# Two moves in the order of a two-layer trunk kernel: the gates at the end of the seventh scan step, the second out-projection round behind the second head's queries and keys

## The chip, the cores and the metric

The kernel runs on one core of a Trainium2 chip. A core has TensorE (PE: matrix products from SBUF into PSUM, with the weight loads shown as PEld), VectorE (DVE), ScalarE (ACT), GpSimd (POOL), and DMA queues; SyncE (SP) and ACT issue the transfers here. Every engine works off its own list of instructions in a fixed order, and semaphores hold an instruction until what it needs is there. The metric is the device time of one execution in microseconds (us); lower is better.

## The reference

A decoder trunk of two residual layers over x with 512 tokens of 1024 channels, in float32. The first layer is a mixer with two halves that read one projection of the normed input: a state-space scan (SSD: 16 heads in 2 groups, with a causal convolution, a decay, a gate z and a norm per group) and a gated linear attention (GLA: 4 heads, with queries, keys, values, a forget gate in the logarithm and an output gate). Both halves go through one output projection. The second layer is latent attention with 16 heads. A dense SwiGLU block follows each. What matters here, cut from the reference:

```python
def ssd_gla_layer(h, w_in, ...):
    z, xbc, dt_raw, q, k, v, g, gk_low = jnp.split(h @ w_in, ...)
    y_ssd = ssd_mixer(z, xbc, dt_raw, ...)        # conv, scan, * silu(z), rms_norm per group of 512
    y_gla = gla_mixer(q, k, v, g, gk_low, ...)
    return jnp.concatenate([y_ssd, y_gla], axis=-1) @ w_out

def gla_mixer(q, k, v, g, gk_low, gk_w2, gk_b, norm_w):
    gk = jax.nn.log_sigmoid(gk_low @ gk_w2 + gk_b) / 16
    gcum = jnp.cumsum(gk over chunks of 64)
    q_dec, k_inv = q * exp(gcum), k * exp(-gcum); k_end = k * exp(g_last - gcum)
    ...  # scores inside a chunk, states across chunks
    return rms_norm(o, norm_w) * silu(g)
```

## The kernel before

Activations lie with channels on the 128 partitions and the 512 tokens along the free axis, so x is eight tiles X[0..7] of 128 x 512. Every dense product is made from three products of a high and a low float32r part (mm3, lines 159 to 162: L160, L161, L162 in the profile), which keeps float32 accuracy. A weight piece is loaded by SP (L148, a buffer of two, wraw), its high part is cast by ACT (L154, whi), its low part subtracted by DVE (L155, wlo; both with three buffers). A product of 128 output channels goes over eight such triples (24 products) into one PSUM bank of the pool acc, which has three banks (NACC); an out-projection piece of 256 columns covers two banks of twelve products each.

The mixer runs in this order of the code:

- Eight scan steps f = 0 to 7 (lines 554 to 579; the eighth is called step 7 and the seventh step 6 here). Each has a conv (L387 to L402: product, L392 scales it into xpad, three taps L397, tanh, and xs at L402), a z gate (L424 to L428 and gate(), L276: zh reads the product), and the core (L430 to L492: decays mt from ACT at L444 and L446, the products L456, L467, L481, L485, and the result y at L491). After step 3 and after step 7 a group norm (L494 to L500 with rstd, L184 to L208) scales the four y of the group and splits them into parts mxh and mxl (L136, L137): the inputs of one out-projection round.
- In step 7, behind the z gate: gates() (L524 to L551) computes the logarithmic forget gates of all GLA heads. It loads a small weight with three DMAs on ACT's queue, splits it, makes four products (L539) into one auxiliary bank, takes Abs (L540), Exp (L543) and Ln (L545) on ACT, the minimum (L541), the difference (L547) and eight running sums (L551) on DVE, and leaves the result in gm. Then comes round 0 of the out-projection (out_round, L296 to L306), which adds 8 banks of products to X (L304), and the values of GLA head 2.
- The GLA heads: inner(h) (L590 to L688) makes queries, keys, scores, states, and the normed output of head h; outer(h) (L690 to L699) multiplies it by the output gate and splits it. Round 1 of the out-projection is called from inside inner(0), behind its queries and keys (after_dense, L636).

The order on each engine is not written out. A scheduler plays the program once when the kernel is built and gives each engine the ready instruction that stands first in the code; weights are ranked 90 instructions (AHEAD) earlier than they stand. Buffers of one tag are handed out in the order of the code. Three things follow that matter around the change. First, gates() borrows buffers of the scan: gw and wt carry the tag cvt of the conv's tanh, w2 the tag cva, and the two ga tiles the tag mt of the decays, each tag with two buffers. Second, the tiles of the heads (pool gla) lie where those of the scan (pool ssd) lay, so the first of them can only be written when the scan's tiles are done with, the group norm's last among them. Third, a round of the out-projection needs PSUM banks of acc, like every dense product.

Of the kernel before, what the change touches and what calls it, by code (L numbers as in the profile page):

```python
# [30 lines left out]
NACC = 3  # L31
PROJ = (0, 2)
R0F = 7


PV = {}
# [12 lines left out]
def kernel(ctx: ExitStack, tc: tile.TileContext, A, yT, stop=99):  # L49
# [11 lines left out]
    def nm(s):  # L61
        cnt[0] += 1
        return f"{s}_{cnt[0]}"

    def acc():
        return pacc.tile([P, T], F32, tag="acc", name=nm("acc"))
# [11 lines left out]
    def aux(tag="st"):  # L78
        while isinstance(phase["tags"][tag], str):
            tag = phase["tags"][tag]  # L80
        return phase["p"].tile([P, T], F32, tag=tag, name=nm(tag), bufs=phase["tags"][tag])
# [23 lines left out]
    def col(name, i=0, lo=0, hi=P):  # L105
        j = PV[name] + i
        return pv[lo:hi, j:j + 1]
# [32 lines left out]
    def weight(src, kc, m):  # L140

        with tc.high_priority(offset=AHEAD):
            return weight_now(src, kc, m)
# [20 lines left out]
    def dense(ps, w, xs):  # L164

        n = len(xs)
        for k, (xh, xl) in enumerate(xs):
            last = mm3(ps, w[0][:, k, :], w[1][:, k, :], xh, xl, k == 0, k == n - 1)
        return last
# [94 lines left out]
    def tok_scalar(R):  # L264

        ps = aux()
        for c in range(4):
            E.transpose(ps[:, c * P:(c + 1) * P], R[:, c * P:(c + 1) * P], ident)
        r = const.tile([P, 4], F32, tag="rtok", name=nm("rtok"))
        V.tensor_copy(r, ps.rearrange("p (c x) -> p c x", c=4)[:, :, 0])  # L270
        return r
# [24 lines left out]
    def out_round(r, parts, nxt=None):  # L296

        for m2 in range(4):
            w = weight(A["w_out"][r, m2], 4, 256)
            for j in range(2):  # L300
                m = 2 * m2 + j
                ps = acc()
                dense(ps, (w[0][:, :, j * P:(j + 1) * P], w[1][:, :, j * P:(j + 1) * P]), parts)
                V.tensor_tensor(X[m], X[m], ps, ALU.add)  # L304
                if nxt is not None:
                    nxt.add(m)  # L306
# [8 lines left out]
    with tc.tile_pool(name="gkp", bufs=1) as gkp:  # L315
# [62 lines left out]
        with tc.tile_pool(name="ssd", bufs=2) as sp:  # L378
# [6 lines left out]
            def conv(i, tag, bufs, bank=acc):  # L385

                w = weight(A["w_xbc"][i], KD, P)  # L387
                ps = bank()
                mm[i] = dense(ps, w, xp)
                xpad = sp.tile([P, T + 3], F32, tag="xpad", name=nm("xpad"))  # L390
                G.memset(xpad[:, 0:3], 0.0)
                V.tensor_tensor(xpad[:, 3:], ps, R, ALU.mult)  # L392
                a = sp.tile([P, T], F32, tag="cva", name=nm("cva"))
                S.activation(a, xpad[:, 3:], AF.Identity, bias=cw[:, 48 + i:49 + i],
                             scale=cw[:, 36 + i:37 + i])
                for k in range(3):
                    V.scalar_tensor_tensor(a, xpad[:, k:k + T], cw[:, 12 * k + i:12 * k + i + 1], a,  # L397
                                           ALU.mult, ALU.add)
                t = sp.tile([P, T], F32, tag="cvt", name=nm("cvt"))
                S.activation(t, a, AF.Tanh)  # L400
                o = sp.tile([P, T], F32, tag=tag, name=nm(tag), bufs=bufs)
                V.scalar_tensor_tensor(o, t, 1.0, a, ALU.add, ALU.mult)  # L402
                return o

            def group(g):

                bank = (lambda: aux("a2")) if g == 0 else acc
                bT = conv(8 + g, "bT", 1, bank)
                cT = conv(10 + g, "cT", 2, bank)
                ps = aux("a1")  # L410
                for c in range(4):
                    E.matmul(ps[:, c * P:(c + 1) * P], bT[:, c * P:(c + 1) * P],
                             cT[:, c * P:(c + 1) * P], start=True, stop=True)
                cb = sp.tile([P, 4, P], F32, tag="cb", name=nm("cb"), bufs=1)
                V.tensor_tensor(cb, ps.rearrange("p (c l) -> p c l", c=4),
                                tri.unsqueeze(1).to_broadcast([P, 4, P]), ALU.mult)
                ps = aux("a1")
                for c in range(3):
                    E.transpose(ps[:, c * P:(c + 1) * P], bT[:, c * P:(c + 1) * P], ident)
                btok = sp.tile([P, 3, P], F32, tag="btok", name=nm("btok"), bufs=1)  # L420
                S.copy(btok, ps[:, :3 * P].rearrange("p (c l) -> p c l", c=3))
                return cb, cT, btok

            def z_gate(f):  # L424
                w = weight(A["w_z"][f], KD, P)
                ps = acc()
                dense(ps, w, xp)
                return gate(sp, "z", ps, R, 2)  # L428
# [65 lines left out]
            def group_norm(g, ys, ssq):  # L494
                Rg = rstd(ssq, 512, sp, "Rg")
                parts = []
                for j, y in enumerate(ys):
                    V.scalar_tensor_tensor(y, y, col("ssd_norm", 4 * g + j), Rg, ALU.mult, ALU.mult)
                    parts.append(to_parts(y))
                return parts  # L500
# [23 lines left out]
            def gates():  # L524

                gw = sp.tile([80, T], F32R, tag="cvt", name="gw")
                G.memset(gw.bitcast(I32), 0)
                w2 = sp.tile([P, T], F32, tag="cva", name="w2")
                wt = sp.tile([P, T], F32R, tag="cvt", name="wt")
                for j in (0, 32, 64):  # L530
                    nc.scalar.dma_start(w2[j:j + 16, :], A["gk_w2"])
                S.copy(wt[0:16, :], w2[0:16, :])
                V.tensor_tensor(gw[0:16, :], w2[0:16, :], wt[0:16, :].bitcast(F32), ALU.subtract)
                for j in (32, 64):
                    S.copy(gw[j:j + 16, :], w2[j:j + 16, :])
                gas = [sp.tile([P, 2, T], F32, tag="mt", name=nm("ga")) for _ in range(2)]
                for h in range(4):
                    ps = aux()
                    E.matmul(ps, gw[:, h * P:(h + 1) * P], gx, start=True, stop=True)  # L539
                    S.activation(gas[h // 2][:, h % 2, :], ps, AF.Abs, bias=col("gk_b", h))  # L540
                    V.tensor_scalar(gm[:, h, :], ps, col("gk_b", h), 0.0, ALU.add, ALU.min)  # L541
                for ga in gas:
                    S.activation(ga, ga, AF.Exp, scale=-1.0)  # L543
                for ga in gas:
                    S.activation(ga, ga, AF.Ln, bias=1.0)  # L545
                for j, ga in enumerate(gas):
                    V.tensor_tensor(gm[:, 2 * j:2 * j + 2], gm[:, 2 * j:2 * j + 2], ga, ALU.subtract)  # L547
                for h in range(4):
                    for t0 in (0, T // 2):
                        gj = gm[:, h, t0:t0 + T // 2]  # L550
                        V.tensor_tensor_scan(gj, rmask, gj, 0.0, ALU.mult, ALU.add)  # L551

            rounds = []
            for f in range(8):
                g = f // 4
                if f % 4 == 0:
                    bc = group(g)
                    ys, ssq = [], None
                xs = conv(f, "xs", 3)
                if f == 0:  # L560
                    with tc.high_priority(offset=STEPS):
                        dt, act, acd = steps(mm[0])
                zg = z_gate(f)
                if f == R0F:
                    gates()
                    out_round(0, rounds[0])
                if f == VALUES[0]:
                    rtok = tok_scalar(R)
                if f in VALUES:
                    values(VALUES.index(f))  # L570
                y = core(f, xs, zg, *bc)
                ys.append(y)
                sq = res.tile([P, T], F32, tag="sq", name=nm("ysq"), bufs=2)
                S.activation(sq, y, AF.Square)
                if ssq is not None:
                    V.tensor_tensor(sq, ssq, sq, ALU.add)
                ssq = sq
                if f % 4 == 3:
                    rounds.append(group_norm(g, ys, ssq))


        with tc.tile_pool(name="gla", bufs=2) as gp:
# [115 lines left out]
                    parts.append(to_parts(os[e]))  # L698
                return parts  # L699

            o0 = inner(0, lambda: out_round(1, rounds[1]))
            o1 = inner(1)
            p01 = outer(0, o0)
            o2 = inner(2)
            p01 += outer(1, o1)
# [56 lines left out]
    with tc.tile_pool(name="mla", bufs=2) as mp, tc.tile_pool(name="mla1", bufs=1) as m1:  # L762
# [41 lines left out]
        for who, n0, n in (("q", 0, 3), ("kv", 3, 2)):  # L804
# [23 lines left out]
            f = rsqrt(m1, lm, [P, 4], "lr", who)  # L828
# [278 lines left out]
```

## Time and profile before

| what | value |
|---|---|
| median of 3 runs | 1379.67 us (1378.09 to 1379.68) |
| the profiled execution: its own time | 1377.99 us |
| its span in the trace | 1375.8 us |
| mean granted clock of TensorE | 0.996 |
| PE busy | 1347.7 us (98%) |
| DVE busy | 814.3 us (59%) |
| ACT busy | 571.5 us (42%) |
| scan steps, gates, round 0 and head queries in the trace | up to about 228 us |
| round 1 in the trace | from 236 us |

How to read it: a row of a timeline is start, duration, engine, line, operation, output and inputs by the program's names, shapes, how many instructions were merged, and in brackets the idle time of the engine before it with what ended it. A start-to-start distance of products is their cost, as their durations overlap. In a waits row, the columns are total us, times, and the longest. Busy shares are means over the whole program, which has stages with very different limits; what a change in one stage is worth is read from that stage.

### The profile page before, as it was taken

How to read it: one execution, taken by the hardware profiler on the slowest of the kernel's cores; microseconds unless marked ns; L12 is line 12 of the kernel's file. 1: busy time of each engine (PE TensorE's matmuls, PEld its weight loads, DVE VectorE, ACT ScalarE, POOL GpSimd, SP SyncE). 2: the span in 40 equal slices, each digit the busy share in tenths (PEclk: the TensorE clock that was granted, in tenths of full speed). 3: DMA queues.
4: the chain of work that ended last, by engine and by line, in shares of the span. 5: the costliest groups of instructions: out<-in, count | busy, mean ns of one | idle time of the engine just before them, and what ended most of it. 6: DMA issues, size and time to landing. Idle time of an engine off the chain costs nothing.

```text
span 1375.8 us, 16690 instructions
## 1 busy us (share of the span) xinstructions
PE 1347.7 (98%) x6506; PEld 1089.3 (79%) x6506; DVE 814.3 (59%) x1369; ACT 571.5 (42%) x950; POOL 7.8 (1%) x35
## 2 busy tenths in 40 slices
PE   9999997999999999999999999999999999999998
PEld 5798886888788888888888887667588888888887
DVE  7877987597768444444333469776594444443221
ACT  7665563344334323223223248774652332332221
POOL 0000000000000000000000000000000000000000
PEclk9999998999999999999999999999999999999999
DMA  5342232222232233233333311111023323333331
GB/s 175 126 138 78 77 98 75 61 62 82 78 102 92 92 100 100 92 104 97 90 90 104 101 60 65 47 47 62 1 92 99 101 92 96 104 92 107 108 105 64
DMA packets 36782, 122.23 MB, mean 89 GB/s; under 512 B 4768, under 2 KB 5792, under 8 KB 36704
## 3 DMA queue, kind: packets, MB, share of 16 engines
q1 hardware_dynamic: 35888, 120.72, 28.1%
q8 instruction: 51, 0.84, 0.3%
q10 hardware_dynamic: 816, 0.46, 0.1%
q14 instruction: 27, 0.22, 0.1%
HBM read 119.03 MB, written 2.13 MB: 88 GB/s over the span
## 4 chain that ended last, share of the span: by engine, by line
PE 91%; DVE 5%; ACT 2%; issue 1%; DMA 0%; SPq 0%; DVEq 0%; ACTq 0%
PE acc L161 27%; PE acc L160 27%; PE acc L162 27%; PE sco L960 2%; PE ptr L974 1%; PE po L983 1%; DVE wlo L155 1%; PE a L481 1%; PE a L673 1%; PE a L467 0%; PE a L662 0%; PE a L485 0%; DMA x<-in_xT_dram 0%; ACT whi L154 0%; PE a L675 0%
## 5 line engine op out<-in xcount | busy, mean ns | idle before, releaser
L154 ACT CAST whi<-wraw 128x1024 fp32r<-128x1024 f32 (+2 forms) x221 | 225.8, 1022 | 556.8 <-PE acc L161 422.8
L160 PE MATMUL acc<-xh,whi 128*128 128x512 f32 x1144 | 448.7, 393 | 2.8 <-ACT qT L943 1.6
L161 PE MATMUL acc<-xl,whi 128*128 128x512 f32 x1144 | 448.6, 392 | 0.0
L162 PE MATMUL acc<-xh,wlo 128*128 128x512 f32 x1144 | 448.0, 392 | 0.0
L155 DVE TENSOR_TENSOR wlo<-wraw,whi 128x1024 fp32r<-128x1024 f32 (+2 forms) x221 | 262.0, 1186 | 155.3 <-ACT whi L154 155.1
L160 PEld LDWEIGHTS acc<-xh,whi 128*128 128x128 f32 x1144 | 214.7, 188 | 48.2 <-ACT qT L943 1.8
L161 PEld LDWEIGHTS acc<-xl,whi 128*128 128x128 f32 x1144 | 214.8, 188 | 45.0 <-issue 1.5
L162 PEld LDWEIGHTS acc<-xh,wlo 128*128 128x128 f32 x1144 | 214.9, 188 | 44.4 <-DVE wlo L155 0.6
L162 PE MATMUL acc<-fhh,wlo 128*128 128x512 f32 x288 | 112.0, 389 | 0.0
L160 PE MATMUL acc<-fhh,whi 128*128 128x512 f32 x288 | 112.0, 389 | 0.0
L161 PE MATMUL acc<-fhl,whi 128*128 128x512 f32 x288 | 112.0, 389 | 0.0
L732 DVE TENSOR_TENSOR fu<-acc,R 128x512 f32<-128x512 f32 x44 | 30.4, 691 | 136.7 <-PE acc L162 136.7
L729 DVE TENSOR_TENSOR fg<-acc,R 128x512 f32<-128x512 f32 x44 | 30.4, 691 | 89.3 <-PE acc L162 89.2
L161 PEld LDWEIGHTS acc<-fhl,whi 128*128 128x128 f32 x288 | 54.1, 188 | 11.3
L160 PEld LDWEIGHTS acc<-fhh,whi 128*128 128x128 f32 x288 | 54.1, 188 | 11.2
L162 PEld LDWEIGHTS acc<-fhh,wlo 128*128 128x128 f32 x288 | 54.1, 188 | 11.1
L160 PE MATMUL acc<-mxh,whi 128*128 128x512 f32 x128 | 51.1, 401 | 7.9 <-ACT mxh L136 7.9
L161 PE MATMUL acc<-mxl,whi 128*128 128x512 f32 x128 | 51.1, 400 | 0.5 <-DVE mxl L137 0.5
L162 PE MATMUL acc<-mxh,wlo 128*128 128x512 f32 x128 | 50.6, 397 | 0.0
L960 PE MATMUL sco<-kT,qT 96*128 96x128 f32 (+3 forms) x128 | 42.8, 445 | 1.5 <-DVE mx L963 1.3
L963 DVE CUSTOM_DVE_ANT_0 sc<-sco,am 128x128 f32<-128x128 f32 (+3 forms) x64 | 30.7, 488 | 13.6 <-PE sco L960 11.5
L965 ACT ACTIVATE sc<-sc,mx 128x128 f32<-128x128 f32 (+3 forms) x64 | 35.7, 561 | 7.3 <-DVE mx L963 6.8
(346 smaller groups left out, 1591.2 us busy)
## 6 DMA issues: line engine op xcount, KB each, us to landing
wraw<-in_w_gate_dram SPq DMA_DIRECT2D x44, 512.0 KB, 3.5
wraw<-in_w_up_dram SPq DMA_DIRECT2D x44, 512.0 KB, 3.5
wraw<-in_w_down_dram SPq DMA_DIRECT2D x32, 512.0 KB, 3.5
wraw<-in_w_out_dram SPq DMA_DIRECT2D x16, 512.0 KB, 3.5
wraw<-in_w_xbc_dram SPq DMA_DIRECT2D x12, 512.0 KB, 3.6
wraw<-in_w_down_dram SPq DMA_DIRECT2D x16, 384.0 KB, 3.1
wraw<-in_w_z_dram SPq DMA_DIRECT2D x8, 512.0 KB, 3.5
wraw<-in_w_v_dram SPq DMA_DIRECT2D x8, 512.0 KB, 3.5
```

The source lines that it names most:

```text
L154: S.copy(hi[:, :kc * m], r)
L155: V.tensor_tensor(lo[:, :kc * m], r, hi.bitcast(F32)[:, :kc * m], ALU.subtract)
L160: E.matmul(out, ah, bh, start=first, stop=False)
L161: E.matmul(out, ah, bl, start=False, stop=False)
L162: return E.matmul(out, al, bh, start=False, stop=last)
L481: E.matmul(pd[64 * h:64 * h + 64, c * P:(c + 1) * P], xdt[:, c, h, :], mt[:, h, c, :], start=True, stop=True)
L673: E.matmul(o, v[:, r, e * P:(e + 1) * P], sc[:, r, :], start=True, stop=(r == 0))
L729: V.tensor_tensor(g, pg, R, ALU.mult)
L732: V.tensor_tensor(u, pu, R, ALU.mult)
L960: E.matmul(ps[:, :n], qts[j][:, b * P:(b + 1) * P], kts[j][:, :n], start=True, stop=True)
L963: V.tensor_tensor_reduce(sc[:, :n], ps[:, :n], am[:, T - n:], -scale, 3e38, ALU.add, ALU.min, mx[:, j:j + 1])
L965: S.activation(sc[:, :n], sc[:, :n], AF.Exp, bias=mx[:, j:j + 1], scale=-1.0, accum_out=sm[:, j:j + 1])
```

## The change

The call of gates() goes from step 7 (between its z gate and round 0) to the end of step 6, behind the sum of its squares and ahead of step 7's conv. Round 1 of the out-projection goes from behind the queries and keys of head 0 to behind those of head 1. Nothing is computed otherwise than before.

```diff
+GATES = 6
...
                 zg = z_gate(f)
                 if f == R0F:
-                    gates()
                     out_round(0, rounds[0])
...
                 ssq = sq
+                if f == GATES:
+                    gates()
                 if f % 4 == 3:
                     rounds.append(group_norm(g, ys, ssq))
...
-            o0 = inner(0, lambda: out_round(1, rounds[1]))
-            o1 = inner(1)
+            o0 = inner(0)
+            o1 = inner(1, lambda: out_round(1, rounds[1]))
             p01 = outer(0, o0)
```

## The prediction

> **What bounds the kernel now.** I read the page first, then the waits of TensorE, then the stretches around the one long wait, and last the order of instructions on each engine there.
>
> ```profile
> span 1375.8 us, 16690 instructions
> PE 1347.7 (98%) x6506; PEld 1089.3 (79%) x6506; DVE 814.3 (59%) x1369; ACT 571.5 (42%) x950; POOL 7.8 (1%) x35
> ```
>
> TensorE (PE) is busy for 98% of the span, and the change adds no product and removes none. So it can only win or lose the time in which PE stands still or runs on a reduced clock. The waits of PE in the first 620 us have one entry that counts:
>
> ```profile
> PE acc L160 <- ACT mxh L136: 7.9, 1, 7.9
> ```
>
> A first product of an out-projection round (it reads mxh) waited 7.9 us for the split of its inputs. The stretches (columns: length; busy time of PE, PEld, DVE, ACT, POOL; granted clock; DMA share; GB/s) show where:
>
> ```profile
> 165.00:180.00 15.00, 15.00 (x86) 12.46 (x86) 14.43 (x27) 5.98 (x11) 0.00 (x0) 1.00 0.24 82
> 180.00:195.00 15.00, 15.00 (x67) 12.28 (x66) 12.34 (x18) 8.95 (x13) 0.52 (x1) 1.00 0.34 112
> 195.00:210.00 15.00, 15.00 (x104) 13.87 (x103) 10.80 (x14) 14.90 (x23) 0.00 (x0) 1.00 0.24 71
> 225.00:240.00 15.00, 6.59 (x20) 4.42 (x19) 12.91 (x20) 3.80 (x6) 0.00 (x0) 0.75 0.24 70
> 240.00:255.00 15.00, 15.00 (x62) 12.27 (x61) 10.80 (x18) 6.20 (x12) 0.99 (x2) 0.91 0.18 49
> ```
>
> Two things are to be seen. From 225 to 240 us PE loses over half the time and then the clock as well. And from 165 to 180 us VectorE (DVE) is 96% busy (14.43 of 15), while it has room from 195 us on. The timeline of PE gives the size of the hole:
>
> ```profile
> 183.35 0.39 PE L160 MATMUL acc<-mxh,whi 128*128 128x512 f32 x1
> ...
> 186.07 0.39 PE L160 MATMUL acc<-mxh,whi 128*128 128x512 f32 x1
> ...
> 216.56 0.91 PE L467 MATMUL a<-xde,btok 128*128 128x128 f32 x6 [0.72 <-DVE xde L462]
> ...
> 227.75 0.39 PE L162 MATMUL acc<-xh,wlo 128*128 128x512 f32 x1
> 236.02 0.79 PE L160 MATMUL acc<-mxh,whi 128*128 128x512 f32 x1 [7.89 <-ACT mxh L136]
> ...
> 242.59 0.52 PE L161 MATMUL acc<-mxl,whi 128*128 128x512 f32 x1
> 242.94 0.39 PE L162 MATMUL acc<-mxh,wlo 128*128 128x512 f32 x1
> ```
>
> The pitch of such a product at full clock is 0.227 us (one bank of twelve, 183.35 to 186.07). The last product of head 0's keys ends its turn at 227.98 (227.75 + 0.23); the second round starts at 236.02: **8.0 us** of standstill. The fourteen products from 236.02 to 242.59 take 6.92 us until 242.94 instead of 3.18: **3.7 us** for the clock and the second short wait. The eighth scan step's state products at 216.56 wait **0.7 us**. Together 12.4 us are lost between 215 and 243 us.
>
> **What holds the second round.** Its inputs come from the norm of scan steps 4 to 7, so from step 7, whose decay tile (mt, two buffers) has to wait until the gates give up the same two buffers. The rows of ScalarE (ACT) in order:
>
> ```profile
> 182.49 1.28 ACTq L531 DMA_DIRECT2D w<-in_gk_w_dram  x3
> ...
> 194.23 1.28 ACT L545 ACT_TABLE_LOAD   x1
> 195.52 1.06 ACT L545 ACTIVATE ga<-ga 128x1024 f32<-128x1024 f32 x1
> ...
> 198.00 1.27 ACT L444 ACTIVATE mt<-acb,act 128x128 f32<-128x128 f32 x4
> ...
> 235.35 1.94 ACT L136 CAST mxh<-y 128x512 fp32r<-128x512 f32 x3 [6.32 <-DVE y L498]
> ```
>
> So from the gates' weight load (182.49) to step 7's first decay (198.00) there are 15.5 us, and from there to the first split input 37.4 us. Step 7 itself (its gate zh at 181.18, quoted below) was waiting for the gates, not for PE.
>
> **The change, part by part.** *Gates earlier* (gates() moves from behind the z gate of step 7 to the end of step 6, ahead of step 7's conv). It issues 3 DMAs on ACT's queue, one clear on POOL, 4 products, about 11 activations with their table loads, and 17 vector operations; none is added. The products (4 of 0.23) are only moved within PE's stream: nothing. The earliest start: their buffers of tags cva and cvt go round by twos in order of the code, and in both versions they come free when an earlier conv has been read:
>
> ```profile
> 168.48 0.69 DVE L402 SCALAR_TENSOR_TENSOR xs<-cvt,cva 128x512 f32<-128x512 f32 x1
> ...
> 181.78 0.68 DVE L402 SCALAR_TENSOR_TENSOR xs<-cvt,cva 128x512 f32<-128x512 f32 x1
> ```
>
> Now it is step 7's conv (181.78 + 0.68 = 182.46, and the DMA goes at 182.49); after the change it is step 6's (169.17). ACT is then in a run of short work, so I take the DMA at about 170.7, that is 11.8 us earlier. Step 7's first decay then comes some 10 us earlier (188), and with the same 37.4 us behind it the first split input is under way at about 225.4, ahead of 227.98. I take the whole 12.4 us as removed.
>
> *What the gates are moved past.* On DVE they now stand ahead of step 7's conv, of zh and of the X additions of the first round. Their cost there:
>
> ```profile
> L551 DVE TENSOR_TENSOR_SCAN gm<-rmask,gm x8: 665/667/683, 198.4 to 211.8; 128x256 f32<-128x256 f32 x8
> L541 DVE TENSOR_SCALAR gm<-st,pv x4: 744/746/753, 191.0 to 201.9; 128x512 f32<-128x512 f32 x4
> L547 DVE TENSOR_TENSOR gm<-gm,ga x2: 1226/1226/1227, 196.6 to 205.8; 128x1024 f32<-128x1024 f32 x2
> L539 PE MATMUL st<-gx,gw x4: 395/397/399, 188.6 to 198.7; 80*128 80x512 f32 x4
> ```
> ```profile
> 175.56 0.86 DVE L473 SCALAR_TENSOR_TENSOR hs<-hs,cd,a 128x64 f32<-128x64 f32 x4
> ...
> 178.31 0.56 DVE L489 TENSOR_TENSOR ea<-a,ea 128x384 f32<-128x384 f32 x1 [0.57 <-PE a L485]
> ...
> 181.18 0.68 DVE L276 SCALAR_TENSOR_TENSOR zh<-acc,R 128x512 f32<-128x512 f32 x1
> ...
> 182.98 1.22 DVE L155 TENSOR_TENSOR wlo<-wraw,whi 128x1024 fp32r<-128x1024 f32 x1
> ...
> 184.72 1.28 DVE L304 TENSOR_TENSOR x<-x,acc 128x512 f32<-128x512 f32 x2
> ...
> 187.05 0.67 DVE L533 TENSOR_TENSOR gw<-w,wt 16x512 fp32r<-16x512 f32 x1
> ```
>
> That is 8 x 0.667 + 4 x 0.746 + 2 x 1.226 + 0.67 = 11.4 us of vector work, now in the stretch that is 96% full. PE feels it through its three product banks: the first round's third bank (183.35) needs zh's read of the z product (done 181.86, 1.5 us in hand), its fourth bank (186.07) needs the first X addition (done about 185.4, 0.7 us in hand). With the DMA at 170.7, and the distances of before (DMA to L533 4.6 us, to the first product 6.1, from one product to the next 3.4), L533, one L541 and the weight split of 182.98 (it moves up too, as its rank is counted back from the round over the gates) come ahead of zh: 0.67 + 0.75 + 1.22 less the 0.57 of idle time at 178.31, 2.1 us against 1.5 in hand: **0.6 us** of stall. Then the first X addition comes up at about 186.3; the first L547 is ready at 185.7 (170.7, plus the 14.1 of before from 182.49 to 196.6, plus 0.9 since L533 finds step 6's state work of 175.56 ahead of it). If it is ahead, it takes 1.2, four scans 2.4 and an L541 0.7 with it, and the stall is **5 us**; if not, it stays at **0.6 to 1**. As the rows put it ahead by half a microsecond, I take 3.5, nearer the upper end. The outer bounds are 0 (all of it falls into idle time) and 11.4 (all 17 stand ahead). Nobody covers such a stall: behind the first round on PE only values(2) could go, and it needs the same banks.
>
> The table load ahead of the first L547 is 1.28 us, and the next activation starts 0.01 us behind it (194.23, 195.52). [...]
>
> *Second round later.* 4 weight DMAs of 512 KB, 8 banks of twelve products and 8 X additions go behind 2 DMAs and 48 products of head 1. PE gets 48 x 0.227 = 10.9 us of work ahead of the round. But those need banks, and there are three: queries 0, keys 0, queries 1 fill them, and keys 1 waits until DVE has read queries 0. That read stands behind the norm, because the gated heads' tiles lie where the scan's lay:
>
> ```profile
> 239.80 0.69 DVE L137 TENSOR_TENSOR mxl<-y,mxh 128x512 fp32r<-128x512 f32 x1 [0.68 <-ACT mxh L136]
> ...
> 240.52 0.69 DVE L606 SCALAR_TENSOR_TENSOR qd<-acc,R 128x512 f32<-128x512 f32 x1
> ```
>
> ```profile
> 240.68 0.99 POOL L588 MEMSET sc<- 128x512 f32 x2 [57.65 <-DVE mxl L137]
> ```
>
> The clear of a gated head's tile, on an engine with nothing else to do, waits for the same split (239.80 + 0.69 = 240.49). So alone, this move covers nothing: see the first rival. With the norm's last split 10 us earlier (230.5), keys 1 (due 227.98 + 24 x 0.227 + 3.5 = 236.9) find their bank free with 6 us in hand, and the move costs nothing; were that hand gone, the price is a stall of the missing time. Head 0's remaining chain, so far behind the second round, now has queries and keys 1 and then the round itself to hide it: 10.9 + 96 x 0.227 = 32.7 us against some 28 (scores at 261.93 to the scaled output):
>
> ```profile
> 261.93 0.28 PE L642 MATMUL a<-qd,ki 128*64 128x64 f32 x2
> ...
> 288.17 1.41 DVE L687 SCALAR_TENSOR_TENSOR o<-o,pv,Ro 128x512 f32<-128x512 f32 x2
> ```
>
> I cost it at nothing. The sum: -12.4 + 3.5 = **-8.9 us**. The profiled execution took 1377.99 (span 1375.8 and 2.2 around it), so 1369.1; the median 1379.67 is 1.7 above that execution, so I expect **1370.8** as a median.
>
> **The rivals.** *The chain isn't shortened.* If step 7 or the norm ends where it did (the gates' buffers come late, or step 7's conv waits for its cvt buffer until the last gate product has read it), keys 1 wait for 240.52 + 0.7 = 241.2, having come up at 227.98 + 5.45 = 233.4: a standstill of 7.8 instead of 8.0, and the same clock. Time 1379.4. For it: the barrier of 240.52; against it: step 7's decay waits for the gates alone. Chance 0.13.
>
> *The stall on the first round is one piece and costs the clock.* A stall of 5 us with the 3.7 of a cold start: -12.4 + 8.7 = -3.7, 1376.0. For it: after 8.0 us the clock was 0.75 and 0.91; against it: split in two, it is short. [...] Chance 0.13.
>
> *The vector queue is overrun (slower).* All 17 operations stand ahead of zh and the X additions, at 165 to 195 us: 11.4, with DVE's waits for the activations inside them as now, and the clock 3.7:
>
> ```profile
> DVE gm L547 <- ACT ga L545: 1.6, 2, 0.9
> ...
> DVE gm L541 <- ACT ga L540: 0.5, 1, 0.5
> ```
>
> 11.4 + 2.1 + 3.7 = 17.2, less 12.4 is +4.8, 1384.5. It is slower from 15.2 us of loss on. For it: 14.43 of 15 busy; against it: the gates' own chain is paced by ACT at 3.4 us a product, which lets zh and some additions through. Chance 0.10.
>
> **How the numbers follow.** The forecast has 0.64, its own range 1367.9 to 1372.3 (stall 0.6 to 5). The range is 1366.5 (no stall, 1367.3, less 0.8, half of the spread of the runs of before) to 1379.5 (the first rival's time). What this kernel's measurement can tell from no change is about 0.2%, 2.8 us. Faster: forecast 0.64 and nearly all of the clock rival, 0.75; same: the first rival and the rest, 0.15; slower: the overrun, 0.10.
>
> **What would show it.** Right: no wait on mxh near 228 us, clock 1.00 throughout 225 to 255, the gates' DMA near 171, the last scan before 203, PE idle 1 to 5 us in 180 to 195 with L304 or L276 as its releaser. Wrong: the gates' DMA still near 182; a PE wait on DVE qd (keys 1) at 233; over 6 us of idle PE at 183 to 195; a new wait behind 240 us in the heads' products, which would mean the head's chain had lost its cover.

## The result, and the profile after

The changed kernel takes 1391.65 us (1390.85 to 1393.13), against 1379.68 for the kernel before on the same chip: a ratio of 1.0089 with a 95% interval of 1.0072 to 1.0107. It is slower, and the time lies outside the range that was forecast. The profiled execution's span went from 1375.8 to 1388.6 us.

The line numbers are one or two higher than before (L155 is now the cast of a weight's high part, L156 its low part, L277 zh, L305 the X addition, L608 the read of the queries). The waits of TensorE in the first 620 us (total us, times, longest):

```profile
PE acc L161 <- ACT cvt L401: 11.6, 1, 11.6
PE acc L161 <- DVE qd L608: 8.0, 1, 8.0
PE acc L163 <- DVE wlo L156: 1.9, 1, 1.9
...
```

There was one wait of 7.9 us, and now there are two long ones and a short one. The timeline of PE shows the places:

```profile
172.37 0.50 PE L163 MATMUL acc<-xh,wlo 128*128 128x512 f32 x1 [1.85 <-DVE wlo L156]
...
185.84 0.39 PE L163 MATMUL acc<-mxh,wlo 128*128 128x512 f32 x1
197.79 0.76 PE L161 MATMUL acc<-mxh,whi 128*128 128x512 f32 x1 [11.57 <-ACT cvt L401]
...
201.75 0.40 PE L161 MATMUL acc<-mxh,whi 128*128 128x512 f32 x1
...
247.71 0.39 PE L163 MATMUL acc<-xh,wlo 128*128 128x512 f32 x1
256.13 0.80 PE L161 MATMUL acc<-xh,whi 128*128 128x512 f32 x1 [8.04 <-DVE qd L608]
...
259.89 0.40 PE L162 MATMUL acc<-xl,whi 128*128 128x512 f32 x1
```

The stretches (the columns as before) show that the granted clock falls twice:

```profile
165.00:180.00 15.00, 13.15 (x77) 10.65 (x76) 14.35 (x26) 9.33 (x16) 0.52 (x1) 1.00 0.27 83
180.00:195.00 15.00, 6.22 (x28) 4.75 (x26) 12.19 (x18) 14.91 (x23) 0.00 (x0) 0.77 0.32 100
195.00:210.00 15.00, 12.21 (x46) 9.94 (x47) 9.54 (x15) 3.25 (x4) 0.00 (x0) 0.78 0.10 25
240.00:255.00 15.00, 8.10 (x35) 6.33 (x35) 13.91 (x21) 4.57 (x6) 0.00 (x0) 0.93 0.19 67
```

Round 0 of the out-projection fills two banks and then stands still at its third, from 186.07 (185.84 + 0.23) to 197.79: 11.7 us. The nine products up to 201.75 take 3.96 us instead of 2.04, so the clock costs 1.9. A product of step 7's z gate had already waited 1.9 for a weight's low part. That is 15.5 us of new loss. The old hole is still there, but one dense product later: keys 1 wait from 247.94 to 256.13, 8.2 us, which is no less than the 8.0 of before. Behind it the pitch is slow up to 259.89 only, and the seven dense products in there take 3.35 us instead of 1.59, so the clock costs about 1.8 and not 3.7; and the wait of 0.7 us of step 7's state products is gone. So the loss of 12.4 went to about 10.0. The sum, 15.5 less 2.4, is 13.1; the span grew by 12.8.

The order on VectorE tells what stood ahead of zh, which reads the bank that round 0 wants third:

```profile
182.21 1.23 DVE L548 TENSOR_TENSOR gm<-gm,ga 128x1024 f32<-128x1024 f32 x1 [1.25 <-ACT ga L546]
...
184.61 2.42 DVE L552 TENSOR_TENSOR_SCAN gm<-rmask,gm 128x256 f32<-128x256 f32 x4
...
192.17 1.23 DVE L548 TENSOR_TENSOR gm<-gm,ga 128x1024 f32<-128x1024 f32 x1 [1.56 <-ACT ga L546]
...
193.97 2.43 DVE L552 TENSOR_TENSOR_SCAN gm<-rmask,gm 128x256 f32<-128x256 f32 x4
...
196.97 0.68 DVE L277 SCALAR_TENSOR_TENSOR zh<-acc,R 128x512 f32<-128x512 f32 x1
197.57 1.27 DVE L305 TENSOR_TENSOR x<-x,acc 128x512 f32<-128x512 f32 x2
```

All of the gates' vector work is done before zh, the last running sum included. The row of waits names an activation (ACT cvt) for the 11.57 us, because that ended last (L401, near 197.7); zh ends at 197.65, 0.1 us before PE goes on. Which of the two it was had to be tried.

The other half is where step 7 stands on PE. The last of the values' products and step 7's transposes, before:

```profile
212.14 0.28 PE L162 MATMUL acc<-whi,xl 128*128 128x256 f32 x1
212.26 0.60 PE L456 MATMUL a<-ident,xs 128*128 128x128 f32 x4
```

and after:

```profile
227.47 0.28 PE L163 MATMUL acc<-whi,xl 128*128 128x256 f32 x1
227.59 0.60 PE L457 MATMUL a<-ident,xs 128*128 128x128 f32 x4
```

In both kernels the transposes come right behind the last product of values(2). After the change step 7's first decay is made at 186.34 (198.00 before), all its decays are ready at 195.97, and VectorE later has so little to do that it is idle for 9 us:

```profile
186.34 0.68 ACT L445 ACTIVATE mt<-acb,act 128x128 f32<-128x128 f32 x2
...
194.91 1.06 ACT L447 ACTIVATE mt<-mt 128x1024 f32<-128x1024 f32 x1
...
249.86 1.94 ACT L137 CAST mxh<-y 128x512 fp32r<-128x512 f32 x3 [0.86 <-DVE y L499]
```
```profile
227.43 1.23 DVE L156 TENSOR_TENSOR wlo<-wraw,whi 128x1024 fp32r<-128x1024 f32 x1 [9.07 <-ACT whi L155]
228.57 0.68 DVE L459 TENSOR_TENSOR xdt<-a,dt 128x512 f32<-128x512 f32 x1
```

So the gates' earlier end did not bring step 7's products forward: in the code, core(7) stands behind round 0 and values(2), and PE's order puts both ahead of it. The first split input is made at 249.86, which is 63.5 us behind the first decay and not 37.4. Everything from the transposes on has moved back with round 0, by 15.3 us at the transposes (212.26 to 227.59) and by 14.9 at the norm's last split (240.49 to 255.36). One product more of cover (24 x 0.227 = 5.45 us) doesn't shorten the wait either, as it meets a later release: round 1 went on with the first split (236.02 before), keys 1 go on with the read of queries 0 behind the last split, which in the kernel before ended at 241.21, 5.2 us later.

### The profile page after: what moved, and what is told of

Same layout as the page of the kernel before. It is cut to its first block, busy times and chain, and to the rows that moved or that the text cites. A ratio compares the mean times of both kernels' runs of the same rounds, so it can differ in the third digit from the quotient of the medians.

```text
span 1388.6 us, 16692 instructions
## 1 busy us (share of the span) xinstructions
PE 1348.2 (97%) x6506; PEld 1089.3 (78%) x6506; DVE 814.0 (59%) x1369; ACT 572.0 (41%) x950; POOL 7.7 (1%) x35
## 4 chain that ended last, share of the span: by engine, by line
PE 88%; DVE 7%; ACT 4%; issue 1%; DMA 1%; SPq 0%; ACTq 0%; DVEq 0%
PE acc L161 26%; PE acc L162 26%; PE acc L163 26%; PE sco L962 2%; PE ptr L976 1%; PE po L985 1%; DVE wlo L156 1%; ACT whi L155 1%; PE a L482 1%; PE a L675 1%; DVE cva L398 0%; PE a L468 0%; ACT xh L243 0%; PE a L677 0%; PE a L486 0%
## 5 line engine op out<-in xcount | busy, mean ns | idle before, releaser
L155 ACT CAST whi<-wraw 128x1024 fp32r<-128x1024 f32 (+2 forms) x221 | 225.8, 1022 | 574.9 <-PE acc L162 456.4
L156 DVE TENSOR_TENSOR wlo<-wraw,whi 128x1024 fp32r<-128x1024 f32 (+2 forms) x221 | 262.0, 1185 | 165.1 <-ACT whi L155 164.8
L161 PE MATMUL acc<-mxh,whi 128*128 128x512 f32 x128 | 50.5, 397 | 11.6 <-ACT cvt L401 11.6
```

What stands on the lines that cost most here:

```text
L155: S.copy(hi[:, :kc * m], r)
L156: V.tensor_tensor(lo[:, :kc * m], r, hi.bitcast(F32)[:, :kc * m], ALU.subtract)
L161: E.matmul(out, ah, bh, start=first, stop=False)
```

## The experiments

The theory (A) is: the gates' vector work, ranked ahead of step 7's conv and z gate, holds the banks of round 0 and makes the whole loss; the hole ahead of round 1 comes from step 7's rank behind the values, and the late round only moves it, since a bank is missing. The rivals are named in the expectations. The edits are against the kernel before or the changed kernel, as said; the ratios are to the kernel before, run beside.

**Each move alone.** The gates alone (against the kernel before):

```diff
+GATES = 6
...
                 if f == R0F:
-                    gates()
                     out_round(0, rounds[0])
...
+                if f == GATES:
+                    gates()
```

> The gates move alone; round 1 stays behind head 0's keys. Theory A (the gates' vector work stands ahead of zh of step 7, and TensorE waits for the bank that zh reads; the hole ahead of round 1 is set by step 7's products, which rank behind the values of head 2, and stays): all of the loss and a little more than in the changed kernel, about 1394 us, with the 11.6 us wait on round 0's third bank and a wait of about 8 us on mxh ahead of round 1. Rival B (the late round makes the second wait, on the read of queries 0): the second wait is gone, about 1382 us.

1397.07 us, ratio 1.0132 (1.0117 to 1.0147). Waits of PE from 100 to 620 us:

```profile
PE acc L161 <- ACT cvt L401: 11.6, 1, 11.6
PE acc L161 <- ACT mxh L137: 7.9, 1, 7.9
PE acc L163 <- DVE wlo L156: 2.5, 1, 2.5
...
```

Both waits stand in full, so the early gates don't shorten the second one and the late round isn't what makes it. Rival B falls. The time is 3 us over the 1394 expected and 5.4 over the changed kernel, though the waits add up to only about 1 us more than there. The rest goes with the clock, whose mean is 0.989 here and 0.993 there: the wait of 2.5 us cost it too (last section), and behind the 7.9 us the pitch stayed slow up to 259.05, for 5.7 us and not 3.8. The late round alone:

```diff
-            o0 = inner(0, lambda: out_round(1, rounds[1]))
-            o1 = inner(1)
+            o0 = inner(0)
+            o1 = inner(1, lambda: out_round(1, rounds[1]))
```

> Round 1 moves alone; the gates stay in step 7. Theory A: no wait in round 0; the 7.9 us wait on mxh turns into a wait of about 8 us of keys 1 on the read of queries 0, which stands behind the group norm: 1377 to 1380 us, no change. Rival B: a loss of about 10 us, 1389. A gain of 9 us or more would show that queries and keys 1 do cover the norm.

1377.7 us, ratio 0.9993 (0.9984 to 1.0003): no difference. The wait:

```profile
PE acc L160 <- DVE qd L606: 8.0, 1, 8.0
```

It is the prediction's first rival: 7.9 us on mxh became 8.0 on the read of queries 0, with 24 products shifted ahead of it.

**What holds round 0.** First the rank of step 7's conv and z gate was raised over the gates, in the changed kernel:

```diff
+RANK = 60
...
-                xs = conv(f, "xs", 3)
+                with tc.high_priority(offset=RANK if f == GATES + 1 else 0):
+                    xs = conv(f, "xs", 3)
...
-                zg = z_gate(f)
+                with tc.high_priority(offset=RANK if f == GATES + 1 else 0):
+                    zg = z_gate(f)
```

> The changed kernel with step 7's conv and z gate ranked 60 instructions earlier, so ahead of the gates in the order of every engine; the gates' place in the code and their buffers stay. Theory A: the 11.6 us wait on round 0's third bank goes to 0 to 3 us, the wait of about 8 us on the read of queries 0 stays: 1377 to 1381 us. Rival C (the row names an activation: ScalarE's table loads and the gates' activations hold the bank or the weights): the wait stays over 8 us, 1388 to 1392.

1388.55 us, ratio 1.0077 (1.0058 to 1.0096). The total lies in Rival C's range, but the wait that Rival C is about is gone. Waits of PE:

```profile
PE acc L162 <- DVE qd L611: 8.0, 1, 8.0
PE acc L162 <- DVE xpad L394: 2.5, 1, 2.5
PE acc L162 <- DVE zh L278: 1.8, 1, 1.8
...
```

The 11.6 us are down to 1.8, and this time the row names zh. But the wrapper, even with an offset of zero, had changed the order in other steps too, with a new wait of 2.5 us at 147 us. That it did so through the ranks of their weights is argued, and not all of the 9 us between this run and the next is accounted for. The clean form wraps step 7 alone:

```diff
+RANK = 60
...
-                xs = conv(f, "xs", 3)
+                if f == GATES + 1:
+                    with tc.high_priority(offset=RANK):
+                        xs = conv(f, "xs", 3)
+                        zg = z_gate(f)
+                else:
+                    xs = conv(f, "xs", 3)
...
-                zg = z_gate(f)
+                if f != GATES + 1:
+                    zg = z_gate(f)
```

> The changed kernel with step 7's conv and z gate alone ranked 60 instructions earlier, ahead of the gates (the run before it wrapped those of all steps and shifted the weights' ranks of the others too, with 2.5 us of new waits before 150 us). Theory A: the wait on round 0's third bank is at most 3 us, the wait of 8 us on the read of queries 0 stays: 1380 to 1384 us. Rival C (ScalarE holds it): still over 8 us of wait in round 0, 1388 or more.

1379.19 us, ratio 1.0004 (0.9994 to 1.0014). The whole loss is gone with the rank of one step, though the gates stand where the change put them. The time is a little under the 1380 to 1384 expected, as the second wait didn't stay at 8.0 but fell to 6.6; why it did was not taken apart. On VectorE zh now comes ahead of the running sums:

```profile
186.57 0.68 DVE L278 SCALAR_TENSOR_TENSOR zh<-acc,R 128x512 f32<-128x512 f32 x1
187.17 1.28 DVE L306 TENSOR_TENSOR x<-x,acc 128x512 f32<-128x512 f32 x2
...
190.48 2.43 DVE L553 TENSOR_TENSOR_SCAN gm<-rmask,gm 128x256 f32<-128x256 f32 x4
```

Waits of PE in it:

```profile
PE acc L162 <- DVE qd L615: 6.6, 1, 6.6
PE st L541 <- DVE gm L543: 1.7, 1, 1.7
```

Then the size was changed: in the changed kernel the gates' last part went back behind step 7's z gate.

```diff
+                return gas
+
+            def sums(gas):
+
                 for j, ga in enumerate(gas):
                     V.tensor_tensor(gm[:, 2 * j:2 * j + 2], gm[:, 2 * j:2 * j + 2], ga, ALU.subtract)
...
                 if f == R0F:
+                    sums(gas)
                     out_round(0, rounds[0])
...
                 if f == GATES:
-                    gates()
+                    gas = gates()
```

> The changed kernel with the last part of the gates, two differences and eight running sums (2 x 1.23 + 8 x 0.67 = 7.8 us of vector work), put back behind step 7's z gate; the products, activations and minima stay at the end of step 6. Theory A (it is vector work ahead of zh that holds round 0's third bank): the 11.6 us wait shrinks by about 7.8, to 2 to 5 us, with the wait of 8 us on the read of queries 0 as before: 1380 to 1384 us. Rival C (ScalarE's activations and table loads, which all stay early): over 8 us, 1388 or more.

1383.44 us, ratio 1.0042 (1.0026 to 1.0058). Waits of PE:

```profile
PE acc L161 <- DVE qd L613: 6.7, 1, 6.7
PE acc L161 <- DVE x L305: 3.1, 1, 3.1
PE acc L163 <- DVE wlo L156: 1.8, 1, 1.8
PE a L457 <- DVE xs L403: 1.7, 1, 1.7
```

The wait in round 0 went from 11.6 to 3.1, 8.5 for 7.8 us of vector work taken out of the way, while ScalarE's part stayed early. So ScalarE alone doesn't hold the bank, and Rival C falls. But ScalarE has a share: in the changed kernel it is busy for 14.91 of the 15 us from 180 to 195, and 2.8 us of VectorE's time ahead of zh are waits for its results (the 1.25 and 1.56 above). With the sums these waits went out of the way as well, so the 8.5 isn't the price of the vector work alone. Some of it came back as 1.7 us at step 7's transposes. Last, the z product was taken off the common banks, in the changed kernel:

```diff
                 w = weight(A["w_z"][f], KD, P)
-                ps = acc()
+                ps = acc() if f < 7 else aux("a1")
```

> The changed kernel with step 7's z product in an auxiliary bank instead of one of the three common ones; every order but that stays. Theory A (TensorE waits for banks that vector reads behind the gates would free, zh's first and then the X additions'): round 0 gets one bank further, 2.7 us of products, and then waits for the first X addition: the wait is 8 to 9.5 us and named L305 or near it, 1388 to 1390 us. If zh's read alone were late, the wait would go altogether: 1378 to 1381.

1391.3 us, ratio 1.0091 (1.0076 to 1.0106). The wait in round 0:

```profile
PE acc L161 <- DVE x L305: 9.8, 1, 9.8
```

Time and wait are a little over the 1388 to 1390 and the 8 to 9.5 us expected, but the mechanism is the one forecast: one bank more, and the next one is held by the first X addition (L305), which stands behind the gates too. It isn't one late read, it is the whole queue of VectorE.

**What makes the hole.** In the kernel before, the values of head 2 go behind step 7's core and norm:

```diff
-                if f in VALUES:
+                if f in VALUES and f != R0F:
                     values(VALUES.index(f))
...
                     rounds.append(group_norm(g, ys, ssq))
+                if f == R0F:
+                    values(VALUES.index(f))
```

> The kernel before, with the values of head 2 put behind step 7's core and its group norm in the code; nothing else moves. Theory A: step 7's transposes and products come ahead of the values, whose 11.6 us then cover the norm together with queries and keys 0: the wait on mxh goes to 0 to 2 us and the clock stays, 1367 to 1371 us. Rival D (the gates hold step 7, as the prediction had it): the wait stays near 8 us, 1379.

1374.23 us, ratio 0.9968 (0.9958 to 0.9979). Waits of PE:

```profile
PE a L467 <- DVE xde L462: 3.1, 1, 3.1
PE acc L161 <- DVE mxl L137: 1.1, 2, 0.8
PE acc L160 <- DVE qd L608: 0.8, 1, 0.8
...
```

The hole ahead of round 1 is gone, without touching the gates: its 7.9 us are down to waits of 0.8 and less. Rival D falls as an account of the hole. Two things close it, and this run doesn't separate them: the norm's last split ends 4.8 us earlier (235.66 against 240.49), and the values' products now run while the norm does. The time is over the 1367 to 1371 expected by some 3 us; step 7's state products now meet a wait of 3.1 us of their own, with the clock at 0.89 behind it. It is here that the gates' place matters, as their running sums stand ahead of xde on VectorE.

The same, with the late round:

> The kernel before with the values of head 2 behind step 7's norm, and round 1 behind head 1's keys. Theory A: the norm now ends before keys 1 need their bank, so the late round does cover what is left: the 2 us of waits at the start of round 1 go, the 3.1 us wait of step 7's state products stays: 1371 to 1373.5 us. Rival E (the late round gives nothing even then): 1374 to 1376.

1372.16 us, ratio 0.9949 (0.9934 to 0.9964). The edit is that of the run just told, with the diff of the late round. Waits of PE:

```profile
PE a L467 <- DVE xde L462: 3.1, 1, 3.1
PE acc L160 <- DVE qd L608: 0.4, 1, 0.4
```

The small waits at the start of round 1 shrank from 2.2 to 0.4. The intervals of the two runs overlap, so that the late round helps here is what the waits say, not the times.

All of it together: the changed kernel, with step 7's conv and z gate ranked over the gates (as in the clean form) and the values behind step 7's norm.

> All of the change (gates at the end of step 6, late round 1), with step 7's conv and z gate ranked ahead of the gates and the values of head 2 behind step 7's norm. Theory A: both long waits are gone, what is left are the short waits of round 0 on the vector queue (2 to 5 us): 1370 to 1377 us. Rival D (the gates' place is what ends the hole): not needed to get there, so a time below that of the run without early gates (1371 to 1373.5) would speak for it.

1369.19 us (1368.31 to 1370.98), ratio 0.9931 (0.9915 to 0.9948), the fastest of all. Waits of PE from 100 to 620 us:

```profile
PE st L541 <- DVE gm L543: 1.7, 1, 1.7
...
```

The wait of step 7's state products is gone, as the gates now end early enough, and the norm's last split lets queries 0 be read at 229.14, not at 255.39 as in the changed kernel or 235.05 as in the run just told:

```profile
228.42 0.69 DVE L139 TENSOR_TENSOR mxl<-y,mxh 128x512 fp32r<-128x512 f32 x1
229.14 0.69 DVE L617 SCALAR_TENSOR_TENSOR qd<-acc,R 128x512 f32<-128x512 f32 x1
```

The time is below that of the run without early gates (1372.16), which speaks for the gates' place counting once step 7's rank is right. The intervals of the two ratios still overlap, so this rests on the wait of 3.1 us that is gone and not on the times. The version with the late sums in place of the rank:

> The run with the late sums and the late round, with the values of head 2 behind step 7's norm as well. Theory A: what holds for the ranked version holds here: no wait over 4 us from 150 to 300 us, 1368 to 1373 us.

1374.43 us, ratio 0.997 (0.996 to 0.998): its own waits in round 0 stayed (3.1 us on the first X addition the longest), and it came out a little over the 1368 to 1373 expected.

**Whether keys 1 want a bank.** The late round alone, with queries 0 and 1 in two auxiliary banks:

```diff
                 w = weight(A["w_q"][h], KD, P)
-                ps = acc()
+                ps = aux(("a1", "a2")[h]) if h < 2 else acc()
```

> The late round alone (gates in step 7), with queries 0 and queries 1 written to two auxiliary banks instead of the three common ones. Theory A (keys 1 stand still for want of a bank while the group norm's tiles hold the gated heads'): keys 1 run on, the wait of 8.0 us shrinks to 0 to 5 us and moves to round 1: 1370 to 1375 us. Rival F (the wait isn't one for a bank): 8 us stay, 1377 to 1379.

1374.25 us, ratio 0.9963 (0.9948 to 0.9977). Waits of PE:

```profile
PE acc L160 <- ACT mxh L136: 2.2, 1, 2.2
PE acc L162 <- DVE wlo L155: 1.0, 1, 1.0
...
```

With the banks, queries and keys 1 do cover the norm, and the 8.0 us fall to 2.2 and some small change: it was the bank. Rival F falls. That the reads wait for the scan's memory, and not for their rank behind the norm alone, was not taken apart.

## Why the prediction was wrong, point by point

- *Where PE loses time, and how much.* Right: PE was the bound, and the hole of 8.0 us with its clock was what could be won. The fastest version wins 0.7% by filling it.
- *What holds the second round.* Wrong, and this is the step that failed first. The prediction had step 7 waiting for the gates and not for PE, moved its decay 10 us earlier and carried the 37.4 us behind it along. The decay did come 11.7 us earlier, but the 37.4 us became 63.5, because the transposes of step 7 stand behind the last product of values(2) in PE's order; the rows at 212.14 and 212.26 of the trace of before show it, and the prediction did not use them. Of the 12.4 us taken as removed, about 2.4 went, and only the 0.7 of step 7's state products fits the forecast mechanism. The wait itself is 8.2 us in place of 8.0. The rest is a shorter slow stretch behind it, which nobody forecast: luck. With the values behind step 7 the hole closes (7.9 to 0.8 us).
- *The gates' start.* Nearly right: forecast 170.7, and as forecast it is step 6's conv that lets them go, but that conv was read sooner. The three loads went at 167.66, 168.03 and 169.42:

```profile
167.66 0.34 ACTq L532 DMA_DIRECT2D w<-in_gk_w_dram  x1
```

- *The stall on round 0.* Right in its mechanism (vector work ahead of zh and the X additions, three banks), wrong in size: 3.5 us forecast, 11.7 measured, with 1.9 of clock and 1.9 for a weight split ahead. The prediction let zh pass after two of the gates' operations, since it paced the gates as they ran before, when they were held up by other work. Ranked higher and started earlier, the first L547 (now L548) ran at 182.21 and not at 185.7, ahead of zh, and VectorE waited inside them (1.25 and 1.56 us in the rows of zh's queue), so that the outer bound of 11.4 was reached. (The gates have 15 vector operations, not 17; the 11.4 is the sum of 15.) Two of the prediction's own signs of being wrong came: over 6 us of idle PE between 183 and 195 us, and keys 1 waiting for the read of queries 0.
- *The late round.* Its cost of nothing was right, and the rival that saw its 10.9 us of cover end after one product, for want of a bank, came out in the run of the late round alone: 7.8 forecast, 8.0 measured. The prediction named this and then counted on the earlier norm to take it away.
- *The rivals.* The overrun of the vector queue, given a chance of 0.10, is what happened: 17.2 us of loss was its price, 15.5 was measured. Its total was still too low (1384.5), as it too took the hole as filled. The slow clock of the second rival came with it, at 1.9 us and not 3.7. What the prediction holds against that rival, that a split stall is short, was its author's estimate; a wait of 2.5 us in the run with the gates alone and one of 3.1 us in the run with step 7 first did go with a clock of 0.89 (last section).
- *Head 0's chain behind the late round.* Right: PE is busy throughout from 270 to 300 us in the changed kernel.

The sum with the measured terms: +15.5 for round 0 and -2.4 for the hole, +13.1, against the span's difference of 12.8.

## What to carry to other kernels

Before counting a chain as shortened, look up where each of its steps stands in the order of every engine it passes: a step that ranks behind work that is always ready gains nothing from an earlier input (here step 7's decay came 11.7 us earlier and its transposes 15.3 us later). Work that is moved earlier in the code is moved ahead of everything on a nearly full engine, so count all of it as a delay of the next read that frees a PSUM bank, and raise that read's rank instead (here VectorE was busy for 14.35 of 15 us from 165 to 180, 11.4 us of the gates' work ahead of zh went with a wait of 11.6 us, and with the rank of step 7 raised it was gone). When the cover is moved, ask whether the covering products have banks to be written to (here 8.0 us of wait without, 2.2 with two auxiliary banks).

## What the runs showed of the hardware

In these runs a wait of TensorE could cost more than itself, and not always the same. Behind 8.0 us (kernel before) the pitch was 0.43 us, where it is 0.227 at a clock of 1.00, for some 6.9 us, with a second wait of 0.5 us among them. Behind 11.7 us (changed kernel) it was so for 4.0 us only, and behind 8.2 us in the same kernel for 3.8. Short waits differ too. Behind a wait of 3.1 us at the same place in the two runs with step 7 first, one run's stretch shows a clock of 0.89 and the other 1.00; first the one with the early round, then the one with the late round:

```profile
210.00:225.00 15.00, 14.03 (x90) 12.34 (x91) 11.17 (x19) 4.26 (x7) 0.00 (x0) 0.89 0.27 76
```
```profile
210.00:225.00 15.00, 14.17 (x97) 12.38 (x98) 12.54 (x22) 4.80 (x8) 0.00 (x0) 1.00 0.32 104
```

In the run with the gates alone a wait of 2.5 us, up to 173.92, cost the clock as well:

```profile
165.00:180.00 15.00, 12.47 (x67) 10.08 (x67) 12.49 (x23) 7.53 (x13) 0.52 (x1) 0.89 0.29 78
```

The wait of 2.5 us at 147 us in the first ranked run did not: the clock is 1.00 there from 140 to 160 us.

So equal waits did not cost the same in these runs (3.1 us: 0.89 and 1.00; 2.5 us: 0.89 and 1.00). What decides whether the clock falls, and for how long, no run here shows.
